# A two-layer transformer block: four tile pairs instead of two at the opening of each FFN, and pools that wait by tile

## The chip, the cores and the metric

The kernel runs on one core of a Trainium2 chip. The metric is the device time of one execution in microseconds; the runs shown are three. The profile is of one further execution.

## The reference

The input is a sequence of 1024 tokens of width 1024 in fp32. Layer 0 mixes with a chunked gMLP and a multi-scale pooling, layer 1 with six heads of differential attention and twelve heads of dilated band attention. Each layer ends in the FFN that the change touches (width 2816), and a final norm closes the block:

```python
def conv_ffn(h, w_up, conv_w, conv_b, w_down):
    a, g = jnp.split(h @ w_up, 2, axis=-1)
    a = lax.conv_general_dilated(a, conv_w, window_strides=(1,), padding=((CONV_WIDTH - 1, 0),),
                                 dimension_numbers=('NWC', 'WIO', 'NWC'), feature_group_count=D_FF) + conv_b
    return (jax.nn.gelu(a) * g) @ w_down
...
        h = h + mix
        h = h + conv_ffn(rms_norm(h, norm_ffn[layer]), ffn_w_up[layer], ffn_conv_w[layer],
                         ffn_conv_b[layer], ffn_w_down[layer])
    return rms_norm(h, final_norm)
```

## The kernel before

Activations are held transposed, features on the 128 partitions and tokens in two halves of 512. Every fp32 operand is split into a high part, rounded by ACT (`A.copy`), and a low part, which DVE subtracts (`V.tensor_sub`); `split` does it for activations, `hi` and `lo` for weights. One product of two 128x128 by 128x512 operands is three matmuls, high by high, low by high and high by low (`mm3`), 512 columns each, added up in one PSUM bank of 128x512 fp32.

**The FFN's up projection** goes over 22 tile pairs j (128 columns of a and of g). Over the two token halves and the two halves of the inner dimension, the eight block products of a pair are brought down to seven (`PRODUCTS`), of 12 matmuls each. Each takes one of four forms of the weights (a itself, two sums of a and g, g itself: `form`, n = 0 to 3) and one operand made from the activations: b11 and b21 from token half 0, and d, e, b22, t3, t4 from sums of both halves. Products 1 and 2 need half 0 alone. Product 1 opens bank x, 2 opens y, 3 opens z; product 4 goes on in x, 5 in z, 6 and 7 in x. Behind a product `read` takes what is needed from the bank: an ACT copy behind 1, 3 and 4, a DVE add behind 2, 5 and 6. `conv` and `gate` close a pair.

**The opening of an FFN.** `out_proj` (and the last projection of the odd mixer in the same way) makes the input h of the FFN tile by tile, with sums of squares for the norm (`Norm.add`). `ff.ahead(i)` makes weight forms early, and `apply(half)` applies the norm: PE adds up over the partitions (ps_n), DVE takes the inverse root (`rsqrt`, twelve small steps n_v to n_rb), PE spreads it over the partitions (ps_b), then DVE scales h and makes the operands: b11 and b21 for half 0, and the seven others for half 1. Then `up` runs products 1 and 2 of pairs 0 and 1, products 3 and 4, 5 and 6, 7 of both, and then pair after pair.

**What sets the order.** Every operation is recorded in program order, and a scheduler lays the records out on the engines by its own estimates; on the chip each engine takes its instructions in that fixed order and waits for semaphores. There are eight PSUM banks: two of pool `ps_mm`, four of `ps_mx`, two of `ps_sm` (norms). In an FFN x takes its bank from `ps_mm`, y and z theirs from `ps_mx`. A pool opened over memory that another pool used makes its first user wait; with `reuse_waits="tile"` it waits for the users of its own bytes, else for the users of the whole pool. The pools of the FFN alone have this mark before. Weight parts come through `wraw_p` (two raw tiles) and `w_tiles` (four pairs of high and low tiles in turn).

Of the kernel before, what the change touches and what calls it, by code (L numbers as in the profile page):

```python
# [60 lines left out]
def tile_block(  # L61
# [22 lines left out]
    const = ctx.enter_context(tc.tile_pool(name="const", bufs=1))  # L84
    dram = ctx.enter_context(tc.tile_pool(name="dram", bufs=1, space=DRAM))
    wraw_p = ctx.enter_context(tc.tile_pool(name="wraw", bufs=2))
    wsp_p = ctx.enter_context(tc.tile_pool(name="wsp", bufs=4))
    hn_p = ctx.enter_context(tc.tile_pool(name="hn", bufs=1))
    ps_mm = ctx.enter_context(tc.tile_pool(name="ps_mm", bufs=2, space=PSUM))
# [174 lines left out]
    class FFN:  # L264
        def __init__(self, layer, stack):
            self.layer = layer
            hp = stack.enter_context(tc.tile_pool(name=f"ffh{layer}", bufs=1, reuse_waits="tile"))
            self.raw_p = stack.enter_context(tc.tile_pool(name=f"ffr{layer}", bufs=4, reuse_waits="tile"))
            self.np = tc.tile_pool(name=f"ffn{layer}", bufs=1, reuse_waits="tile")
# [84 lines left out]
        def form(self, j, n, part):  # L354

            if part == 1:
                return self.lo(j, n)
            if n == 0:
                self.raw(j)
            f = self.forms[j]  # L360
            a, g = f["a"], f["g"]
            c0, c1 = slice(0, HF), slice(HF, S)
            if n == 0:
                self.hi(j, 0, a)
            elif n == 1:
# [2 lines left out]
                V.tensor_add(q[:, c1], q[:, c0], a[:, c0])
# [37 lines left out]
        def read(self, j, n, st):  # L406

            ep = self.ep

            def copy(key, bank):  # L410
                st[key] = ep.tile([P, HF], F32, tag="sb", name=f"f_{key}", bufs=5)
                A.copy(st[key], st[bank])  # L412

            if n == 1:
                copy("x1", "x")
            elif n == 2:
                st["a"] = ep.tile([P, P + S], F32, tag="f_a", name="f_a", bufs=2)
                G.memset(st["a"][:, 0:2], 0.0)
                V.tensor_tensor(st["a"][:, 2 : 2 + HF], st["y"], st["x1"], op=ALU.add)
            elif n == 3:  # L420
                copy("z1", "z")
            elif n == 4:
                copy("u2", "x")
            elif n == 5:
                V.tensor_tensor(st["a"][:, 2 + HF : 2 + S], st["z"], st["u2"], op=ALU.add)
            elif n == 6:
                st["g1"] = ep.tile([P, HF], F32, tag="sb", name="f_g1", bufs=5)
                V.tensor_tensor(st["g1"], st["x"], st["z1"], op=ALU.add)
# [10 lines left out]
        def gate(self, j):  # L439
            st = self.st.pop(j)  # L440
            acc = st["acc"]
            V.scalar_tensor_tensor(acc[:, :HF], acc[:, :HF], -1.0, st["x"], op0=ALU.mult, op1=ALU.mult)
            V.scalar_tensor_tensor(acc[:, HF:], acc[:, HF:], -1.0, st["g1"], op0=ALU.mult, op1=ALU.mult)
            nc.sync.dma_start(a_dram[j], acc)

        def up(self):
            self.st = {}

            both = (0, 1)
            for n in (1, 2):  # L450
                for j in both:
                    self.product(j, n)
# [138 lines left out]
    def odd_mixer():  # L591
        stack = ExitStack()
        with stack:
            ent = stack.enter_context
            qk_p = ent(tc.tile_pool(name="od_qk", bufs=2))
            st_p = ent(tc.tile_pool(name="od_st", bufs=1))
            op = ent(tc.tile_pool(name="od", bufs=1))
            wk = ent(tc.tile_pool(name="od_wk", bufs=2))
            sm = ent(tc.tile_pool(name="od_sm", bufs=4))
            ps_sc = ent(tc.tile_pool(name="ps_sc", bufs=3, space=PSUM))  # L600
            ps_sm = ent(tc.tile_pool(name="ps_s3", bufs=3, space=PSUM))
# [626 lines left out]
```

## Time and profile before

| what | value |
|---|---|
| three runs | 2395.47, 2397.24 and 2398.65 us, median 2397.24 |
| profiled execution | 2396.34 us, span 2394.6, granted clock 0.988 |
| PE | busy 2307.8 us, 96% of the span |
| DVE | busy 1552.0 us, 65% |
| ACT | busy 954.8 us, 40% |
| DMA | 221.60 MB, mean 93 GB/s |
| both FFN openings | about 265 to 305 and 1685 to 1760 us |

A row of the timeline has the start, the duration shown, the engine, the line, the operation, the tiles out and in, and in brackets the idle time before it with what ended it. The duration of a matmul overlaps the next one's, so its cost is read from start to start.

### The profile page before, as it was taken

The page shows a single profiled execution, that of the slowest core. Times are in us where ns is not written, and L with a number is a line of the kernel's source. Part 1 is how long each engine was busy: PE and PEld are TensorE (multiplying, and loading weights), DVE is VectorE, ACT ScalarE, POOL GpSimd, SP SyncE. Part 2 cuts the span into 40 slices and gives each one's busy share as a digit, 9 for nine tenths or more (in the row PEclk, how much of TensorE's full clock was granted, in tenths as well). Part 3 has the DMA queues.
Part 4 walks back from the last instruction along what each step waited for, and adds up shares of the span by engine and source line. Part 5 has one row for each costly group of instructions (what it writes and reads, how often), then busy time and mean ns, then how long its engine had stood idle before and what let it go on. Part 6 is the DMA issues. An engine that isn't in the chain of part 4 may idle for free.

```text
span 2394.6 us, 30695 instructions
## 1 busy us (share of the span) xinstructions
PE 2307.8 (96%) x11652; PEld 1948.4 (81%) x11652; DVE 1552.0 (65%) x2957; ACT 954.8 (40%) x1549; POOL 9.2 (0%) x67
## 2 busy tenths in 40 slices
PE   7999899999999998999999999999699999999997
PEld 7888688888888887898888888878578888888887
DVE  6663976666674447355544788896986666675446
ACT  6231433343441113445544555663444333341111
POOL 0000000000000000000000000000000000000000
PEclk9999999999999999999999999999899999999998
DMA  4114132222273213122122131233322222263211
GB/s 139 62 55 165 36 97 88 79 80 80 88 244 107 89 50 108 55 76 79 60 69 73 37 103 54 75 124 135 134 89 88 88 80 80 86 235 119 88 36 71
DMA packets 174067, 221.60 MB, mean 93 GB/s; under 512 B 11104, under 2 KB 121952, under 8 KB 173920
## 3 DMA queue, kind: packets, MB, share of 16 engines
q1 hardware_dynamic: 173056, 218.61, 28.0%
q8 instruction: 91, 1.49, 0.3%
q10 hardware_dynamic: 864, 1.04, 0.2%
q14 instruction: 56, 0.46, 0.1%
HBM read 160.79 MB, written 52.53 MB: 89 GB/s over the span
## 4 chain that ended last, share of the span: by engine, by line
PE 82%; DVE 9%; ACT 4%; DMA 3%; issue 2%; SPq 0%; DVEq 0%; ACTq 0%
PE ps_d L163 7%; PE ps_d L164 7%; PE ps_d L165 7%; PE ps_x L163 6%; PE ps_x L165 6%; PE ps_x L164 6%; PE ps_z L165 3%; PE ps_z L164 3%; PE ps_z L163 3%; PE ps_qk L163 3%; PE ps_qk L165 3%; PE ps_qk L164 3%; PE ps_o L165 2%; PE ps_o L163 2%; PE ps_o L164 2%
## 5 line engine op out<-in xcount | busy, mean ns | idle before, releaser
L163 PE MATMUL ps_d<-hph,wh 128*128 128x512 f32 (+1 forms) x736 | 279.8, 380 | 0.0
L164 PE MATMUL ps_d<-hpl,wh 128*128 128x512 f32 (+1 forms) x736 | 279.7, 380 | 0.0
L165 PE MATMUL ps_d<-hph,wl 128*128 128x512 f32 (+1 forms) x736 | 279.6, 380 | 0.0
L544 DVE TENSOR_TENSOR x<-ps_d,x 128x512 f32<-128x512 f32 (+1 forms) x200 | 131.9, 666 | 184.9 <-PE ps_d L165 184.7
L134 DVE TENSOR_TENSOR wl<-raw,wh 128x1024 fp32r<-128x1024 f32 (+1 forms) x110 | 131.9, 1200 | 172.7 <-ACT wh L133 172.5
L133 ACT CAST wh<-raw 128x1024 fp32r<-128x1024 f32 (+1 forms) x110 | 113.3, 1036 | 261.8 <-PE ps_d L164 177.3
L348 ACT CAST wh<-q 128x1024 fp32r<-128x1024 f32 x88 | 92.4, 1050 | 247.9 <-PE ps_z L164 218.9
L352 DVE TENSOR_TENSOR wl<-q,wh 128x1024 fp32r<-128x1024 f32 x88 | 107.6, 1224 | 126.7 <-ACT wh L348 126.7
L165 PEld LDWEIGHTS ps_d<-hph,wl 128*128 128x128 f32 x736 | 138.4, 188 | 26.4
L163 PEld LDWEIGHTS ps_d<-hph,wh 128*128 128x128 f32 x736 | 138.4, 188 | 26.3
L164 PEld LDWEIGHTS ps_d<-hpl,wh 128*128 128x128 f32 x736 | 138.4, 188 | 25.9
L163 PE MATMUL ps_qk<-hph,wh 128*128 128x512 f32 x384 | 151.9, 396 | 0.0
L165 PE MATMUL ps_qk<-hph,wl 128*128 128x512 f32 x384 | 151.6, 395 | 0.0
L164 PE MATMUL ps_qk<-hpl,wh 128*128 128x512 f32 x384 | 151.5, 394 | 0.0
L163 PE MATMUL ps_z<-hph,wh 128*128 128x512 f32 x352 | 139.0, 397 | 7.1 <-ACT hph L174 6.6
L163 PE MATMUL ps_x<-x,wh 128*128 128x512 f32 x352 | 137.3, 391 | 4.8 <-ACT f_u L412 4.8
L165 PE MATMUL ps_z<-hph,wl 128*128 128x512 f32 x352 | 139.3, 396 | 1.0 <-DVE wl L352 1.0
L164 PE MATMUL ps_z<-hpl,wh 128*128 128x512 f32 x352 | 139.5, 396 | 0.7 <-DVE hpl L175 0.7
L164 PE MATMUL ps_x<-x,wh 128*128 128x512 f32 x352 | 137.3, 390 | 1.0 <-DVE x L175 1.0
L165 PE MATMUL ps_x<-x,wl 128*128 128x512 f32 x352 | 136.8, 389 | 0.0
L163 PE MATMUL ps_vv<-wh,hph 128*128 128x256 f32 x384 | 110.2, 287 | 10.2 <-ACT qk L660 10.2
L164 PE MATMUL ps_vv<-wl,hph 128*128 128x256 f32 x384 | 110.7, 288 | 0.0
(268 smaller groups left out, 5511.4 us busy)
## 6 DMA issues: line engine op xcount, KB each, us to landing
wr<-in_w_up SPq DMA_DIRECT2D x88, 512.0 KB, 4.1
a_dram<-h SPq DMA_DIRECT2D x44, 512.0 KB, 2.6
ar<-a_dram SPq DMA_DIRECT2D x44, 512.0 KB, 4.6
raw<-in_w_dn SPq DMA_DIRECT2D x44, 512.0 KB, 4.5
raw<-in_w_oin SPq DMA_DIRECT2D x36, 512.0 KB, 3.7
h_dram<-h SPq DMA_DIRECT2D x32, 256.0 KB, 4.8
x<-h_dram SPq DMA_DIRECT2D x32, 256.0 KB, 5.2
raw<-in_w_ein SPq DMA_DIRECT2D x12, 512.0 KB, 4.4
```

Of the source, the lines that this page charges most:

```text
L133: A.copy(wh, raw)
L134: V.tensor_sub(wl, raw, wh.bitcast(F32))
L163: T.matmul(ps, lh, rh, start=first, stop=False, skip_group_check=more)
L164: T.matmul(ps, lh, rl, start=False, stop=False, skip_group_check=more)
L165: T.matmul(ps, ll, rh, start=False, stop=last, skip_group_check=more)
L348: A.copy(t[0], src)
L352: V.tensor_sub(l, src, h.bitcast(F32))
L544: V.tensor_tensor(h, ps, h, op=ALU.add)
```

## The change

Each FFN opens with products 1 and 2 of four tile pairs. `early` names pairs 2 and 3; `ahead(1)` loads their a half once more, ahead of time, and makes form 0 of them, while forms 1 of pairs 0 and 1 are now made in `up`, behind products 1 and 2. The six banks of `ps_mm` and `ps_mx` are taken once and go round in a list (`banks`): a bank comes back to it when y, z or x has been read by DVE. A tile f_s takes the place of f_x, f_z, f_u and f_g, and pairs 2 and 3 keep the sum of y there until ACT copies it into f_a (`open_a`), two copies for each FFN. All pools wait by tile.

```diff
--- before.py
+++ after.py
@@ -81,12 +81,15 @@
     nc = tc.nc
     V, A, G, T = nc.vector, nc.scalar, nc.gpsimd, nc.tensor
 
-    wraw_p = ctx.enter_context(tc.tile_pool(name="wraw", bufs=2))
...
-    ps_mm = ctx.enter_context(tc.tile_pool(name="ps_mm", bufs=2, space=PSUM))
+    def pool(name, **kw):
+        return tc.tile_pool(name=name, reuse_waits="tile", **kw)
+
+    wraw_p = ctx.enter_context(pool(name="wraw", bufs=2))
...
+    ps_mm = ctx.enter_context(pool(name="ps_mm", bufs=2, space=PSUM))
 
 
     ident = const.tile([P, P], F32, name="ident")
@@ -338,10 +341,12 @@
 
         def raw(self, j):
             f = self.forms[j] = {}
-            src = w_up[self.layer, j].rearrange("p (k x c) -> p k x c", x=2, c=P)
             for i, x in enumerate("ag"):
                 f[x] = self.raw_p.tile([P, 1024], F32, tag="wr", name="wr")
-                nc.sync.dma_start(f[x].rearrange("p (k c) -> p k c", c=P), src[:, :, i, :])
+                nc.sync.dma_start(f[x].rearrange("p (k c) -> p k c", c=P), self.columns(j, i))
+
+        def columns(self, j, i):
+            return w_up[self.layer, j].rearrange("p (k x c) -> p k x c", x=2, c=P)[:, :, i, :]
 
         def hi(self, j, n, src):
             t = self.forms[j][n] = [x[:, : src.shape[-1]] for x in w_tiles()] + [src]
@@ -355,7 +360,7 @@
 
             if part == 1:
                 return self.lo(j, n)
-            if n == 0:
+            if j not in self.forms or n == 1 and j in self.early:
                 self.raw(j)
             f = self.forms[j]
             a, g = f["a"], f["g"]
@@ -379,9 +384,19 @@
             self.form(j, n, 0)
             self.form(j, n, 1)
 
+        early = (2, 3)
+
         def ahead(self, i):
-            for j in range(2):
-                self.forms_of(j, i)
+
+            for j in (2 * i, 2 * i + 1):
+                if j not in self.early:
+                    self.forms_of(j, 0)
+                    continue
+                a = wraw_p.tile([P, 1024], F32, tag="raw", name="a")
+                nc.sync.dma_start(a.rearrange("p (k c) -> p k c", c=P), self.columns(j, 0))
+                self.forms[j] = {}
+                self.hi(j, 0, a)
+                self.lo(j, 0)
 
 
         PRODUCTS = {
@@ -394,8 +409,7 @@
             tile_n, block, b, opens = self.PRODUCTS[n]
             bank = {2: "y", 3: "z", 5: "z"}.get(n, "x")
             if opens:
-                st[bank] = ps_mm.tile([P, HF], F32, tag="mm", name="ps_x") if n == 1 else ps_mx.tile(
-                    [P, HF], F32, tag="mx", name=f"ps_{bank}")
+                st[bank] = self.banks.pop(0)
             wh, wl, _ = self.forms[j][tile_n]
             bh, bl = self.B[b]
             for k in range(4):
@@ -406,26 +420,30 @@
         def read(self, j, n, st):
 
             ep = self.ep
-
-            def copy(key, bank):
-                st[key] = ep.tile([P, HF], F32, tag="sb", name=f"f_{key}", bufs=5)
-                A.copy(st[key], st[bank])
-
-            if n == 1:
-                copy("x1", "x")
+            if n in (1, 3):
+                st[n] = ep.tile([P, HF], F32, tag="sb", name=f"f_s{n}", bufs=6)
+                A.copy(st[n], st["x" if n == 1 else "z"])
             elif n == 2:
-                st["a"] = ep.tile([P, P + S], F32, tag="f_a", name="f_a", bufs=2)
-                G.memset(st["a"][:, 0:2], 0.0)
-                V.tensor_tensor(st["a"][:, 2 : 2 + HF], st["y"], st["x1"], op=ALU.add)
-            elif n == 3:
-                copy("z1", "z")
+
+                if j not in self.early:
+                    self.open_a(j)
+                to = st[1] if j in self.early else st["a"][:, 2 : 2 + HF]
+                V.tensor_tensor(to, st["y"], st[1], op=ALU.add)
+                self.banks.append(st["y"])
             elif n == 4:
-                copy("u2", "x")
+                A.copy(st[1], st["x"])
             elif n == 5:
-                V.tensor_tensor(st["a"][:, 2 + HF : 2 + S], st["z"], st["u2"], op=ALU.add)
+                V.tensor_tensor(st["a"][:, 2 + HF : 2 + S], st["z"], st[1], op=ALU.add)
+                self.banks.append(st["z"])
             elif n == 6:
-                st["g1"] = ep.tile([P, HF], F32, tag="sb", name="f_g1", bufs=5)
-                V.tensor_tensor(st["g1"], st["x"], st["z1"], op=ALU.add)
+                V.tensor_tensor(st[3], st["x"], st[3], op=ALU.add)
+
+        def open_a(self, j):
+            st = self.st[j]
+            st["a"] = self.ep.tile([P, P + S], F32, tag="f_a", name="f_a", bufs=2)
+            G.memset(st["a"][:, 0:2], 0.0)
+            if j in self.early:
+                A.copy(st["a"][:, 2 : 2 + HF], st[1])
 
         def conv(self, j):
             st, a = self.st[j], self.st[j]["a"]
@@ -440,16 +458,24 @@
             st = self.st.pop(j)
             acc = st["acc"]
             V.scalar_tensor_tensor(acc[:, :HF], acc[:, :HF], -1.0, st["x"], op0=ALU.mult, op1=ALU.mult)
-            V.scalar_tensor_tensor(acc[:, HF:], acc[:, HF:], -1.0, st["g1"], op0=ALU.mult, op1=ALU.mult)
+            self.banks.append(st["x"])
+            V.scalar_tensor_tensor(acc[:, HF:], acc[:, HF:], -1.0, st[3], op0=ALU.mult, op1=ALU.mult)
             nc.sync.dma_start(a_dram[j], acc)
 
         def up(self):
             self.st = {}
+            self.banks = [ps_mm.tile([P, HF], F32, tag="mm", name=f"ps_u{i}") for i in range(2)]
+            self.banks += [ps_mx.tile([P, HF], F32, tag="mx", name=f"ps_u{i + 2}") for i in range(4)]
 
             both = (0, 1)
-            for n in (1, 2):
-                for j in both:
-                    self.product(j, n)
+            for j in both:
+                self.product(j, 1)
+                self.product(j, 2)
+            for j in both:
+                self.forms_of(j, 1)
+            for j in self.early:
+                self.product(j, 1)
+                self.product(j, 2)
             for j in both:
                 self.forms_of(j, 2)
             for n in (3, 4):
@@ -462,8 +488,8 @@
                     self.product(j, n)
                     if n == 5:
                         self.conv(j)
-                    else:
-                        self.forms_of(2, j)
+                    elif j == 1:
+                        self.forms_of(2, 1)
             for j in both:
                 self.product(j, 7)
                 self.gate(j)
@@ -472,13 +498,17 @@
                 nxt = j + 1 if j + 1 < NFF else None
 
                 def form(n, part):
-                    if nxt is not None:
+                    if nxt is not None and not (n == 0 and nxt in self.early):
                         self.form(nxt, n, part)
 
-                self.product(j, 1)
+                if j in self.early:
+                    self.open_a(j)
+                else:
+                    self.product(j, 1)
                 if j > 2:
                     self.form(j, 3, 1)
-                self.product(j, 2)
+                if j not in self.early:
+                    self.product(j, 2)
                 if j > 2:
                     self.gate(j - 1)
                 form(0, 0)
...
@@ -592,13 +622,13 @@
-            qk_p = ent(tc.tile_pool(name="od_qk", bufs=2))
-            ps_sc = ent(tc.tile_pool(name="ps_sc", bufs=3, space=PSUM))
+            qk_p = ent(pool(name="od_qk", bufs=2))
+            ps_sc = ent(pool(name="ps_sc", bufs=3, space=PSUM))
...
```

PE in the second FFN, around the spreading of the norm (ps_b). In ps_x, ps_y, ps_z the letter names the bank's use; ps_u0 to ps_u5 are the six banks; hph and hpl are operands b11, b21 (half 0: _0) and d, b22 (_1), x_0 and x_1 are parts of e. Before:

```order
L209 MATMUL ps_n_14732<-narrow_77,nsum_14631 128x1 x4
L218 MATMUL ps_b_14754<-ident_72,n_rb_14752 128x128 x4
L163 MATMUL ps_z_14877<-hph_0_1_83,wh_14721 128x512
L163 MATMUL ps_z_14892<-hph_0_1_83,wh_14728 128x512
L164 MATMUL ps_z_14877<-hpl_0_1_91,wh_14721 128x512
...
L163 MATMUL ps_z_14877<-hph_1_1_85,wh_14721 128x512
...
L163 MATMUL ps_x_14803<-x_0_0_14599,wh_14721 128x512
L163 MATMUL ps_x_14818<-x_0_0_14599,wh_14728 128x512
...
L164 MATMUL ps_x_14803<-x_1_0_14601,wh_14721 128x512
```

and now:

```order
L168 MATMUL ps_u5_14708<-hph_3_0_88,wl_14623 128x512
L221 MATMUL ps_b_14654<-ident_72,n_rb_14652 128x128 x4
L166 MATMUL ps_u0_14703<-x_0_0_14501,wh_14770 128x512
L166 MATMUL ps_u2_14705<-x_0_0_14501,wh_14777 128x512
L167 MATMUL ps_u0_14703<-x_1_0_14503,wh_14770 128x512
...
L167 MATMUL ps_u2_14705<-x_1_0_14503,wh_14777 128x512
...
L167 MATMUL ps_u0_14703<-x_1_1_14504,wh_14770 128x512
...
L166 MATMUL ps_u1_14704<-hph_0_0_82,wh_14628 128x512
...
L166 MATMUL ps_u3_14706<-hph_2_0_86,wh_14628 128x512
...
L166 MATMUL ps_u5_14708<-hph_0_1_83,wh_14770 128x512
```

Ahead of the change product 3 (hph_0_1 into ps_z) of pairs 0 and 1 stood behind ps_b, and product 4 (x_0_0 into ps_x) behind it. Now product 4 stands there, then products 1 and 2 of pair 3 on the banks u1 and u3, which held y of pairs 0 and 1, and then product 3.

DVE in the second FFN, at the end of apply(1), before:

```order
L335 SCALAR_TENSOR_TENSOR h_3_0_14428<-h_1_0_14424,h_3_0_14428 128x1024
L175 TENSOR_TENSOR h_2_1_14791<-h_2_0_14426,h_0_1_14789 128x1024
L419 TENSOR_TENSOR f_a_14846<-ps_y_14833,f_x1_14816 128x512
L175 TENSOR_TENSOR h_3_1_14792<-h_3_0_14428,h_1_1_14790 128x1024
L419 TENSOR_TENSOR f_a_14862<-ps_y_14849,f_x1_14831 128x512
L352 TENSOR_TENSOR wl_14936<-wr_14558,wh_14935 128x512
```

and now:

```order
L338 SCALAR_TENSOR_TENSOR h_3_0_14330<-h_1_0_14326,h_3_0_14330 128x1024
L178 TENSOR_TENSOR h_2_1_14691<-h_2_0_14328,h_0_1_14689 128x1024
L431 TENSOR_TENSOR f_a_14735<-ps_u1_14704,f_s1_14721 128x512
L178 TENSOR_TENSOR h_3_1_14692<-h_3_0_14330,h_1_1_14690 128x1024
L431 TENSOR_TENSOR f_a_14764<-ps_u3_14706,f_s1_14750 128x512
L431 TENSOR_TENSOR f_s1_14793<-ps_u5_14708,f_s1_14793 128x512
```

The adds that read y of pairs 0 and 1 (L419, now L431) kept their place in the queue, between and behind the last low halves; one more, for pair 2, came behind them.

PE in the first FFN, around ps_b, before:

```order
L164 MATMUL ps_y_2370<-hpl_3_0_96,wh_2183 128x512
L218 MATMUL ps_b_2291<-ident_72,n_rb_2289 128x128 x4
L165 MATMUL ps_y_2370<-hph_3_0_88,wl_2184 128x512
...
L165 MATMUL ps_y_2386<-hph_3_0_88,wl_2192 128x512
L163 MATMUL ps_z_2414<-hph_0_1_83,wh_2258 128x512
L163 MATMUL ps_z_2429<-hph_0_1_83,wh_2265 128x512
L164 MATMUL ps_z_2414<-hpl_0_1_91,wh_2258 128x512
...
L163 MATMUL ps_x_2340<-x_0_0_2095,wh_2258 128x512
```

and now:

```order
L167 MATMUL ps_u3_2341<-hpl_3_0_96,wh_2191 128x512
L221 MATMUL ps_b_2289<-ident_72,n_rb_2287 128x128 x4
L168 MATMUL ps_u3_2341<-hph_3_0_88,wl_2192 128x512
...
L166 MATMUL ps_u4_2342<-hph_0_0_82,wh_2257 128x512
...
L166 MATMUL ps_u5_2343<-hph_2_0_86,wh_2257 128x512
...
L166 MATMUL ps_u0_2338<-x_0_0_2095,wh_2405 128x512
L166 MATMUL ps_u2_2340<-x_0_0_2095,wh_2412 128x512
L167 MATMUL ps_u0_2338<-x_1_0_2097,wh_2405 128x512
...
L166 MATMUL ps_u1_2339<-hph_0_0_82,wh_2263 128x512
...
L166 MATMUL ps_u3_2341<-hph_2_0_86,wh_2263 128x512
...
L166 MATMUL ps_u5_2343<-hph_0_1_83,wh_2405 128x512
```

Before, ps_b stood one matmul ahead of the end of pair 0's product 2 (ps_y_2370), with pair 1's (ps_y_2386) behind it. Now it stands within pair 1's product 2 (ps_u3); products 1 and 2 of pair 2 (u4, u5) come behind, and then the order is as in the second FFN.

More of the change, by code (lines that the diff above doesn't have):

```diff
@@ L82, in tile_block @@
     V, A, G, T = nc.vector, nc.scalar, nc.gpsimd, nc.tensor
[L84 to L89 removed]
+    def pool(name, **kw):
+        return tc.tile_pool(name=name, reuse_waits="tile", **kw)
+    const = ctx.enter_context(pool(name="const", bufs=1))
+    dram = ctx.enter_context(pool(name="dram", bufs=1, space=DRAM))
+    wraw_p = ctx.enter_context(pool(name="wraw", bufs=2))
+    wsp_p = ctx.enter_context(pool(name="wsp", bufs=4))
+    hn_p = ctx.enter_context(pool(name="hn", bufs=1))
+    ps_mm = ctx.enter_context(pool(name="ps_mm", bufs=2, space=PSUM))
     ident = const.tile([P, P], F32, name="ident")
@@ L266, in __init__ @@
             self.layer = layer
-            hp = stack.enter_context(tc.tile_pool(name=f"ffh{layer}", bufs=1, reuse_waits="tile"))
-            self.raw_p = stack.enter_context(tc.tile_pool(name=f"ffr{layer}", bufs=4, reuse_waits="tile"))
-            self.np = tc.tile_pool(name=f"ffn{layer}", bufs=1, reuse_waits="tile")
+            hp = stack.enter_context(pool(name=f"ffh{layer}", bufs=1))
+            self.raw_p = stack.enter_context(pool(name=f"ffr{layer}", bufs=4))
+            self.np = pool(name=f"ffn{layer}", bufs=1)
             self.tile = lambda x, m, h, t: hp.tile([P, 2, HF], t, tag=f"{x}{m}{h}", name=f"{x}_{m}_{h}")
@@ L562, in run @@
             self.np.__exit__(None, None, None)
-            with tc.tile_pool(name=f"ffe{self.layer}", bufs=1, reuse_waits="tile") as self.ep:
+            with pool(name=f"ffe{self.layer}", bufs=1) as self.ep:
                 self.up()
-            with tc.tile_pool(name=f"ffm{self.layer}", bufs=1, reuse_waits="tile") as np_:
+            with pool(name=f"ffm{self.layer}", bufs=1) as np_:
                 norm = Norm(np_)
@@ L594, in odd_mixer @@
             ent = stack.enter_context
-            qk_p = ent(tc.tile_pool(name="od_qk", bufs=2))
[L596 to L599, printed above, removed]
-            ps_sc = ent(tc.tile_pool(name="ps_sc", bufs=3, space=PSUM))
-            ps_sm = ent(tc.tile_pool(name="ps_s3", bufs=3, space=PSUM))
+            qk_p = ent(pool(name="od_qk", bufs=2))
+            st_p = ent(pool(name="od_st", bufs=1))
+            op = ent(pool(name="od", bufs=1))
+            wk = ent(pool(name="od_wk", bufs=2))
+            sm = ent(pool(name="od_sm", bufs=4))
+            ps_sc = ent(pool(name="ps_sc", bufs=3, space=PSUM))
+            ps_sm = ent(pool(name="ps_s3", bufs=3, space=PSUM))
             cosT = op.tile([P, HF], F32, name="cosT")
@@ L961, in tile_block @@
     banks = ExitStack()
-    ps_mx = banks.enter_context(tc.tile_pool(name="ps_mx0", bufs=4, space=PSUM))
-    ps_sm = banks.enter_context(tc.tile_pool(name="ps_sm0", bufs=2, space=PSUM))
+    ps_mx = banks.enter_context(pool(name="ps_mx0", bufs=4, space=PSUM))
+    ps_sm = banks.enter_context(pool(name="ps_sm0", bufs=2, space=PSUM))
     QT = HF // 2
     even = ExitStack()
-    evr = even.enter_context(tc.tile_pool(name="ev_r", bufs=1))
+    evr = even.enter_context(pool(name="ev_r", bufs=1))
     r_row = [evr.tile([P, HF], F32, name=f"r_row{h}") for h in range(2)]
@@ L973, in tile_block @@
         for q in range(4):
-            xp = x0.enter_context(tc.tile_pool(name=f"x{q}", bufs=1))
+            xp = x0.enter_context(pool(name=f"x{q}", bufs=1))
             xt.append([xp.tile([P, QT], F32, name=f"x_{q}_{kt}") for kt in range(KT)])
-        nrm = Norm(x0.enter_context(tc.tile_pool(name="x_n", bufs=1)))
+        nrm = Norm(x0.enter_context(pool(name="x_n", bufs=1)))
         for q in range(4):
@@ L993, in tile_block @@
             V.tensor_copy(r_col[:, q * 2 : q * 2 + 2], y[:, :2])
-    with tc.tile_pool(name="ev_v", bufs=1) as evv, tc.tile_pool(name="ev", bufs=1) as ev, tc.tile_pool(
+    with pool(name="ev_v", bufs=1) as evv, pool(name="ev", bufs=1) as ev, pool(
         name="ev2", bufs=2
@@ L1130, in tile_block @@
     with ExitStack() as stack:
-        ps_mx = stack.enter_context(tc.tile_pool(name="ps_mx1", bufs=4, space=PSUM))
-        ps_sm = stack.enter_context(tc.tile_pool(name="ps_sm1", bufs=2, space=PSUM))
+        ps_mx = stack.enter_context(pool(name="ps_mx1", bufs=4, space=PSUM))
+        ps_sm = stack.enter_context(pool(name="ps_sm1", bufs=2, space=PSUM))
         ff = FFN(1, stack)
```

## The prediction

> **What bounds the kernel now.** I read the page's busy shares and its chain of waits first, then windows of 60 us side by side, then the rows of PE, DVE and ACT in the windows that fall short. The rows are the busy line, the chain's shares by engine, and three windows: the opening of the first FFN, the opening of the second, and a steady stretch of an FFN (columns: PE, PEld, DVE, ACT, POOL busy us and count, granted clock, DMA share, GB/s).
>
> ```profile
> PE 2307.8 (96%) x11652; PEld 1948.4 (81%) x11652; DVE 1552.0 (65%) x2957; ACT 954.8 (40%) x1549; POOL 9.2 (0%) x67
> PE 82%; DVE 9%; ACT 4%; DMA 3%; issue 2%; SPq 0%; DVEq 0%; ACTq 0%
> 240.00:300.00 60.00, 50.73 (x216) 39.33 (x216) 55.32 (x84) 26.71 (x32) 0.36 (x2) 0.94 0.11 36
> 1680.00:1740.00 60.00, 41.28 (x164) 32.24 (x164) 56.73 (x90) 26.04 (x32) 0.20 (x2) 0.80 0.33 109
> 1800.00:1860.00 60.00, 60.00 (x267) 49.67 (x266) 38.91 (x47) 23.18 (x28) 0.30 (x3) 1.00 0.25 79
> ```
>
> PE sets the end wherever it has work: the steady window is full, and 267 matmuls in it give about 0.227 us each, start to start. The two openings are the places where PE waits, and there DVE is the busy one (55.32 and 56.73 of 60). So the change is worth what it does to PE's waits in two stretches, at about 265 to 305 us and 1705 to 1760 us. First PE in the second opening (a bracket is idle time before the row and what ended it; the last two rows group 1705 to 1760 by line, with the idle time behind the second bar):
>
> ```profile
> 1706.25 1.02 PE L209 MATMUL ps_n<-narrow,nsum 128*128 128x1 f32 x8 [1.28 <-DVE nsum L202]
> 1715.37 2.04 PE L218 MATMUL ps_b<-ident,n_rb 128*128 128x128 f32 x8 [8.09 <-DVE n_rb L215]
> 1722.20 1.22 PE L163 MATMUL ps_z<-hph,wh 128*128 128x512 f32 x2 [4.79 <-ACT hph L174]
> 1725.02 0.63 PE L164 MATMUL ps_z<-hpl,wh 128*128 128x512 f32 x1
> 1726.30 0.63 PE L163 MATMUL ps_z<-hph,wh 128*128 128x512 f32 x1
> 1727.31 0.40 PE L164 MATMUL ps_z<-hpl,wh 128*128 128x512 f32 x1
> 1754.62 0.50 PE L163 MATMUL ps_x<-h,wh 128*128 128x512 f32 x1 [1.00 <-DVE f_g L428]
> ...
> L163 PE MATMUL ps_z<-hph,wh 128*128 128x512 f32 x17 | 7.8, 469 | 5.2 <-ACT hph L174 4.8 <-ACT wh L348 0.5
> L164 PE MATMUL ps_z<-hpl,wh 128*128 128x512 f32 x17 | 7.5, 442 | 0.2 <-DVE hpl L175 0.2
> ```
>
> The matmuls of products 1 and 2 for two tile pairs end at 1704.97 (1706.25 less 1.28). PE then waits 1.28 + 8.09 + 5.2 + 0.2 + 1.00 = 15.8 us. After a wait matmuls start 0.43 us apart (1725.02 to 1726.30 is three steps), until about 1726.9, ten of them: a slow stretch costs 10 x 0.20 = 2.0 us. ps_b itself took 2.04 where the warm one below takes 1.05. In all 15.8 + 2.0 + 1.0 = 18.8 us are lost here. Now what DVE and ACT do at that time:
>
> ```profile
> 1705.43 0.68 DVE L202 TENSOR_TENSOR nsum<-nsum,nsq 128x512 f32<-128x512 f32 x1
> 1706.03 0.68 DVE L368 TENSOR_TENSOR q<-q,wr 128x512 f32<-128x512 f32 x1
> 1707.32 0.16 DVE L212 TENSOR_SCALAR n_v<-ps_n 128x4 f32<-128x4 f32 x1 [0.60 <-PE ps_n L209]
> 1714.80 0.42 DVE L215 COPY n_rb<-n_y 128x512 f32<-128x512 f32 x1
> 1717.88 2.06 DVE L309 SCALAR_TENSOR_TENSOR h<-h,narrow,ps_b 128x512 f32<-128x512 f32 x3
> 1729.96 1.21 DVE L175 TENSOR_TENSOR x<-h,x 128x1024 fp32r<-128x1024 f32 x1
> 1734.50 1.21 DVE L175 TENSOR_TENSOR x<-h,x 128x1024 fp32r<-128x1024 f32 x1
> 1742.45 0.68 DVE L419 TENSOR_TENSOR f_a<-ps_y,f_x 128x512 f32<-128x512 f32 x1
> 1744.18 0.67 DVE L419 TENSOR_TENSOR f_a<-ps_y,f_x 128x512 f32<-128x512 f32 x1
> 1728.28 1.06 ACT L174 CAST x<-h 128x1024 fp32r<-128x1024 f32 x1 [1.59 <-DVE h L326]
> ```
>
> Call D the start of the first scaling behind ps_b (L309, 1717.88). From D on DVE works through apply(1) without a pause. The operand of product 4 has its high half at D+11.5 (1728.28 + 1.06), its low halves at D+13.3 (1729.96 + 1.21) and D+17.8 (1734.50 + 1.21). The two adds that read the y banks end at D+25.25 and D+27.0. Before the change nobody waits for these adds, since products 3 and 4 have banks of their own.
>
> **The change part by part, second FFN.** It adds 24 matmuls of tile pair 2 ahead of ps_b and 24 of pair 3 behind it; they are moved from later, PE's count is the same. There are six banks. Pairs 0, 1 and 2 take all six, and pair 3 opens on the banks of y of pairs 0 and 1, that is behind the two adds, which DVE still has at the end of its apply(1) queue. Behind pair 3 in PE's order stands product 3 of pairs 0 and 1, which ran at D+4.3 before. So three things move.
>
> (a) ps_n stands behind 16 of the moved matmuls: 1704.97 + 16 x 0.227 = 1708.6, so n_v comes at 1709.7 in place of 1707.32. Between n_v and n_rb DVE now has one 128x512 add more (0.6 us, 1705.43 to 1706.03). n_rb and D move by 2.4 + 0.6 = 3.0 us, D to 1720.9. PE is busy to 1704.97 + 5.45 + 1.02 = 1711.4 and waits to 1718.4 (1715.37 + 3.0): 6.9 us, and 1.0 for a slow ps_b.
>
> (b) From ps_b's end (1720.4) PE has two matmuls until D+13.3, at 1734.2: 13.3 us of waiting and a slow stretch of 2.0. The rest of product 4 (22 matmuls, ten of them slow) then runs to D+20.3; the second low half at D+17.8 is in time.
>
> (c) From D+20.3 to D+25.25 PE waits for pair 0's y bank: 4.95, and 2.0 for slow matmuls. Then 48 matmuls run without a stop; the second bank (D+27.0) is in time.
>
> Sum 6.9 + 1.0 + 13.3 + 2.0 + 4.95 + 2.0 = 30.2 against 18.8: **+11.4 us**. From below: D does not move (-3) and neither wait makes matmuls slow (-4), +4.4. From above: DVE's forms wait for casts once more (1 us), and the y add of pair 3 or a late weight costs one 128x1024 step or two (1.2 each), +15.
>
> **First FFN.** PE, DVE and ACT in its opening, and the window of its loss:
>
> ```profile
> 269.33 1.05 PE L218 MATMUL ps_b<-ident,n_rb 128*128 128x128 f32 x8
> 275.20 0.73 PE L163 MATMUL ps_z<-hph,wh 128*128 128x512 f32 x2 [1.86 <-ACT hph L174]
> 288.65 0.50 PE L164 MATMUL ps_x<-x,wh 128*128 128x512 f32 x1 [1.02 <-DVE x L175]
> 296.74 0.78 PE L163 MATMUL ps_x<-x,wh 128*128 128x512 f32 x1 [4.00 <-ACT f_u L412]
> 298.93 0.80 PE L165 MATMUL ps_z<-hph,wl 128*128 128x512 f32 x1 [0.98 <-DVE wl L352]
> 272.00:305.00 33.00, 23.86 (x79) 16.88 (x79) 30.86 (x33) 14.87 (x18) 0.00 (x0) 0.84 0.08 25
> 264.83 0.16 DVE L212 TENSOR_SCALAR n_v<-ps_n 128x4 f32<-128x4 f32 x1 [0.90 <-PE ps_n L209]
> 268.62 0.43 DVE L215 COPY n_rb<-n_y 128x512 f32<-128x512 f32 x1
> 270.42 2.06 DVE L309 SCALAR_TENSOR_TENSOR h<-h,narrow,ps_b 128x512 f32<-128x512 f32 x3 [1.37 <-PE ps_b L218]
> 282.84 1.22 DVE L175 TENSOR_TENSOR x<-h,x 128x1024 fp32r<-128x1024 f32 x1
> 287.38 1.22 DVE L175 TENSOR_TENSOR x<-h,x 128x1024 fp32r<-128x1024 f32 x1
> 295.33 0.68 DVE L419 TENSOR_TENSOR f_a<-ps_y,f_x 128x512 f32<-128x512 f32 x1
> 296.10 0.58 ACT L412 COPY f_u<-ps_x 128x512 f32<-128x512 f32 x1 [0.69 <-DVE f_a L419]
> ```
>
> Lost before: 33.0 - 79 x 0.227 = 15.1 us. After it, D = 270.42 moves: between n_v and n_rb DVE gets one low split more (1.2) and two adds (0.6 each), and I allow 0.3 for a weight cast that has to wait for its buffer: 2.7 in all, D = 273.1. Here pair 2's 24 matmuls and the last 4 of pair 1 stand behind ps_b: 28 x 0.227 = 6.4, to D+6.4. Then PE waits for product 4's low half (282.84 + 1.22, D+13.6) with two matmuls between: 6.8, and 2.0 slow; for the second low half (D+18.2) 1.6; then from D+19.6 for the y bank (295.33 + 0.68, D+25.6) 6.0, and 2.0 slow; 0.4 ahead of ps_b. Sum 18.8, less 15.1: **+3.7 us**. The 4.00 wait for f_u goes, since the f_ copies get six slots and no new one is taken there. From below, with no slow matmuls behind the two waits, 0; from above, with a second cast wait moving D by two steps and the first 24 matmuls late by as much, +8.
>
> The clock can be weighed otherwise. The Trainium skill ("TensorE: Matmul & The Clock Gate", Part 1, What's actually happening) has it that a cold start lasts about 3.4 us by a free-running window, with 6 to 14 slow matmuls seen. By that page four stretches of 1.2 to 2.8 us would make the whole sum about 3 us less or more; the trace's ten matmuls, 2.0 us, lie in between and are used.
>
> **What is hidden.** Two 512 KB loads of a weight half for each FFN issue well ahead, where the DMA share is 0.11 to 0.33; uncovered, one would delay a cast, in the upper ends above. Two ACT copies more for each FFN, of the size of f_u, lie on an engine that is busy 26 of 60 us: 0, and 1.2 us uncovered. **Pools that wait by tile**: the largest wait beside a pool is the one ahead of attention.
>
> ```profile
> 961.97 0.58 PE L163 MATMUL ps_vv<-wh,hph 128*128 128x256 f32 x1 [10.17 <-ACT qk L660]
> 960.81 0.62 ACT L174 CAST hph<-n_t 128x512 fp32r<-128x512 f32 x1 [0.82 <-DVE n_t L227]
> 961.34 1.06 ACT L660 COPY qk<-ps_qk 128x512 f32<-128x512 f32 x2
> ```
>
> The copy comes right behind ACT's last cast of the norm, and in ACT's order it stands behind it after the change too. So the pool's wait frees nothing: 0, and 0.8 us of gain as the bound (one wait of the norm, 0.82).
>
> Total +11.4 + 3.7 = +15.1. The profiled execution took 2396.34 (span 2394.6 and 1.74 around it), 0.9 below the median of 2397.24: 2411.4 there, **2412 us** as a median. The ends: +4.4 + 0 - 0.8 = +3.6 and +15 + 8 = +23, from 2400 to 2420.
>
> **The rivals.**
>
> *The added products fill the waits* (faster). If pair 3's matmuls too ran in the idle time, 48 x 0.227 = 10.9 us would go into the 8.09 + 4.79 of the second FFN, and the waits 1.86 + 1.02 + 4.00 + 0.98 = 7.9 of the first would be filled: 2397.2 - 18.8 = 2378. For it: the idle time is there. Against it: the banks, freed at D+25; and product 3, the work that fills D+4.3 to D+11.5 today, stands behind them. It decides if the y adds run before apply(1). The Trainium skill ("Perfetto Trace Analysis", Optimizing Tensor Performance, Matmuls) says that independent groups should rotate through banks so that the emptying of one overlaps the next group's matmuls, which is what this rival counts on; in the steady window the trace agrees, 60.00 of 60 with the banks in rotation. Chance 0.08.
>
> *DVE sets the end of the opening anyway* (no change). DVE is busy 56.73 of 60 and the change moves its instructions without adding any; if PE's later work waits for DVE to empty its queue, what PE misses costs nothing: 2397. Against it: behind 1744 PE runs full (60.00 of 60), so matmuls owed at D+25 are paid for. Chance 0.08.
>
> *The pools free the attention's start*: 10.2 less, 2412 - 10.2 = 2402. Against it ACT's order. Chance 0.06.
>
> **How the numbers follow.** Forecast 0.78, rivals 0.08, 0.08 and 0.06. The range 2400 to 2420 holds the forecast with its bounds and the third rival, about 8 in 10. Under 0.2% (4.8 us) this measurement can't tell a change: faster 0.09 (the first rival and a rest), same 0.11 (the second and half of the third), slower 0.80.
>
> **What would show it.** In the profile after: a wait of about 13 us on PE behind ps_b in the second opening, ended by the low half of x, then one of about 5 ended by DVE's add at L431 ahead of ps_u; in the first opening two waits of about 6 to 7 with the same enders; n_rb 3 us later against the rows around it; the 10.17 us ahead of ps_vv unchanged. I am wrong if pair 3's matmuls start before D+20, if product 3 runs ahead of them, or if the window from D+30 on still has waits that hide the loss.

## The result and the profile after

The changed kernel takes 2411.35 us in the median (2410.45 to 2413.09), the kernel before 2397.8 (2395.47 to 2398.65). The ratio is 1.0059 with a 95% interval of 1.0042 to 1.0076: slower by 0.6%, 14 us. One execution among all those below, in the run with three pairs and two banks emptied by ACT, took 9481 us and is left out of its ratio. The profiled executions differ by as much, with spans of 2408.7 and 2394.6.

The windows of the two openings, of the kernel after. The second window is taken 4 us later than the same one of before, since the same row of DVE (the last of the four low halves of half 0, L178) starts 4.14 us later there; columns as in the prediction.

```profile
262.00:322.00 60.00, 46.56 (x188) 36.53 (x187) 46.82 (x66) 21.25 (x26) 0.00 (x0) 0.86 0.13 40
1700.00:1770.00 70.00, 46.56 (x184) 37.00 (x184) 54.13 (x76) 25.89 (x31) 0.00 (x0) 0.80 0.10 31
```

and of the kernel before:

```profile
262.00:322.00 60.00, 50.86 (x206) 39.42 (x205) 54.44 (x74) 25.59 (x31) 0.56 (x4) 0.91 0.19 60
1696.00:1766.00 70.00, 54.24 (x226) 42.90 (x225) 65.97 (x89) 35.07 (x41) 0.40 (x4) 0.88 0.20 60
```

PE gets through 18 matmuls less in the first opening and 42 less in the second. At 0.227 us these are 4.1 and 9.5 us. In the whole run PE and DVE have the same instructions as before and ACT four copies more; here each is less busy. PE's lost time is the time from the start of each matmul to the next one's, less what it takes at full speed. Added up over all matmuls of the trace it grows from 15.7 to 20.4 us in the first opening (240 to 400 us), from 28.1 to 38.5 in the second (1675 to 1900), and falls by 1.0 in all the rest: 14.1.

PE in the second opening, after:

```profile
1712.33 0.95 PE L212 MATMUL ps_n<-narrow,nsum 128*128 128x1 f32 x8
1721.66 2.05 PE L221 MATMUL ps_b<-ident,n_rb 128*128 128x128 f32 x8 [6.42 <-DVE n_rb L218]
1735.25 1.22 PE L166 MATMUL ps_u<-x,wh 128*128 128x512 f32 x2 [11.54 <-ACT x L177]
1737.10 0.79 PE L167 MATMUL ps_u<-x,wh 128*128 128x512 f32 x1 [0.63 <-DVE x L178]
1749.05 0.80 PE L166 MATMUL ps_u<-hph,wh 128*128 128x512 f32 x1 [4.86 <-DVE f_a L431]
```

and DVE at the same time:

```profile
1703.08 1.22 DVE L178 TENSOR_TENSOR hpl<-h,hph 128x1024 fp32r<-128x1024 f32 x1
1713.31 0.16 DVE L215 TENSOR_SCALAR n_v<-ps_n 128x4 f32<-128x4 f32 x1 [1.92 <-PE ps_n L212]
1721.08 0.43 DVE L218 COPY n_rb<-n_y 128x512 f32<-128x512 f32 x1
1723.74 2.06 DVE L312 SCALAR_TENSOR_TENSOR h<-h,narrow,ps_b 128x512 f32<-128x512 f32 x3 [2.23 <-PE ps_b L221]
1748.32 0.68 DVE L431 TENSOR_TENSOR f_a<-ps_u,f_s 128x512 f32<-128x512 f32 x1
1757.46 0.69 DVE L431 TENSOR_TENSOR f_s<-ps_u,f_s 128x512 f32<-128x512 f32 x1 [4.80 <-PE ps_u L168]
```

Here D is 1723.74. The add of pair 0's y starts at D+24.6, 1748.32, at the end of DVE's queue of apply(1), and PE takes up pair 3 in that bank as soon as it is through. Later DVE itself waits 4.80 us for PE (the last row): what PE did not do in time, DVE cannot read.

The first opening, after, on PE:

```profile
271.53 1.13 PE L221 MATMUL ps_b<-ident,n_rb 128*128 128x128 f32 x8 [0.25 <-DVE n_rb L218]
284.40 1.22 PE L166 MATMUL ps_u<-x,wh 128*128 128x512 f32 x2 [5.38 <-ACT x L177]
290.80 0.50 PE L167 MATMUL ps_u<-x,wh 128*128 128x512 f32 x1 [1.19 <-DVE x L178]
298.21 0.80 PE L166 MATMUL ps_u<-hph,wh 128*128 128x512 f32 x1 [5.99 <-DVE f_a L431]
```

The same two waits: for product 4's operand, then for the bank that DVE's add holds.

### The profile page after: what moved, and what is told of

Read it like the earlier page. It is cut to its first block, busy times and chain, and to the rows that moved or that the text cites. A ratio compares the mean times of both kernels' runs of the same rounds, so it can differ in the third digit from the quotient of the medians.

```text
span 2408.7 us, 30648 instructions
## 1 busy us (share of the span) xinstructions
PE 2309.5 (96%) x11652; PEld 1950.2 (81%) x11652; DVE 1551.8 (64%) x2957; ACT 958.4 (40%) x1553; POOL 9.4 (0%) x67
## 4 chain that ended last, share of the span: by engine, by line
PE 82%; DVE 8%; ACT 4%; DMA 3%; issue 2%; SPq 0%; DVEq 0%; ACTq 0%
PE ps_u L166 12%; PE ps_u L168 12%; PE ps_u L167 12%; PE ps_d L166 6%; PE ps_d L167 6%; PE ps_d L168 6%; PE ps_qk L167 3%; PE ps_qk L168 3%; PE ps_qk L166 3%; PE ps_o L166 2%; PE ps_o L168 2%; PE ps_o L167 2%; PE ps_vv L166 2%; PE ps_vv L168 2%; PE ps_vv L167 2%
## 5 line engine op out<-in xcount | busy, mean ns | idle before, releaser
L166 PE MATMUL ps_u<-hph,wh 128*128 128x512 f32 x768 | 302.2, 394 | 14.4 <-DVE f_a L431 10.8
L168 PE MATMUL ps_u<-hph,wl 128*128 128x512 f32 x768 | 301.9, 393 | 0.3 <-DVE wl L357 0.3
L167 PE MATMUL ps_u<-hpl,wh 128*128 128x512 f32 x768 | 301.7, 393 | 0.0
L166 PEld LDWEIGHTS ps_u<-hph,wh 128*128 128x128 f32 x768 | 146.1, 190 | 45.6 <-DVE f_a L431 11.7
L168 PEld LDWEIGHTS ps_u<-hph,wl 128*128 128x128 f32 x768 | 145.7, 190 | 31.2 <-DVE wl L357 0.8
L167 PEld LDWEIGHTS ps_u<-hpl,wh 128*128 128x128 f32 x768 | 146.0, 190 | 30.6
L166 PE MATMUL ps_u<-x,wh 128*128 128x512 f32 x352 | 138.7, 396 | 16.9 <-ACT x L177 16.9
L167 PE MATMUL ps_u<-x,wh 128*128 128x512 f32 x352 | 138.9, 395 | 2.4 <-DVE x L178 2.4
```

What stands on the lines that cost most here:

```text
L166: T.matmul(ps, lh, rh, start=first, stop=False, skip_group_check=more)
L167: T.matmul(ps, lh, rl, start=False, stop=False, skip_group_check=more)
L168: T.matmul(ps, ll, rh, start=False, stop=last, skip_group_check=more)
```

## The experiments

The theory: three pairs take all six banks, so the next product that opens one has to take a bank of y, which DVE empties at the end of its queue of apply(1); in PE's fixed order that product, and product 3 behind it, hold up the rest. The rivals: the pools; the amount of work that is moved forward, with what it adds to DVE ahead of n_rb; the copies and the list of banks. Each run has its median, and beside it the kernel before was run on the same chip; the ratio is of these two sets of runs, with its 95% interval, and can differ in the last digits from that of the medians.

### The pools alone

The kernel before, with `reuse_waits="tile"` on every pool:

```diff
+    def pool(name, **kw):
+        return tc.tile_pool(name=name, reuse_waits="tile", **kw)
-    const = ctx.enter_context(tc.tile_pool(name="const", bufs=1))
+    const = ctx.enter_context(pool(name="const", bufs=1))
...
```

> Only the pools: the kernel before, with every pool waiting by tile; the FFN openings as before. My theory (the loss is made in the two openings, by the order of PE around ps_b): no difference, 2397 to 2399 us, and the 10.17 us wait of PE ahead of ps_vv stays. The rival that the pools cost time or give it back: 2392 or less if they free the start of attention or of the even mixer, 2404 or more if they carry part of the 14 us.

Measured: 2398.29 us, ratio 1.0007 (0.9999 to 1.0016). The wait ahead of attention, in this run:

```profile
963.12 0.58 PE L166 MATMUL ps_vv<-wh,hph 128*128 128x256 f32 x1 [10.19 <-ACT qk L663]
```

It is as long as before (10.17): the pool's wait was behind ACT's order and freed nothing. The pools are worth nothing that can be told.

### The opening alone

```diff
     def pool(name, **kw):
-        return tc.tile_pool(name=name, reuse_waits="tile", **kw)
+        if name.startswith("ff"):
+            kw["reuse_waits"] = "tile"
+        return tc.tile_pool(name=name, **kw)
```

> Only the opening: the changed kernel with the pools outside the FFN waiting by whole pool again. My theory: all of the loss stays, 2410 to 2413. The rival that pools carry part: nearer to 2398 by that part.

Measured: 2413.03 us, ratio 1.0068 (1.0055 to 1.0080). The whole loss is in the opening; this and the run of the pools give the two parts of the change apart.

### Two pairs, with the list of banks

The changed kernel with the opening narrowed:

```diff
-        early = (2, 3)
+        early = ()
...
                 if j not in self.early:
-                    self.forms_of(j, 0)
+                    if j < 2:
+                        self.forms_of(j, 0)
                     continue
...
-                    elif j == 1:
-                        self.forms_of(2, 1)
+                    elif j == 1 or 2 not in self.early:
+                        self.forms_of(2, j)
```

> The changed kernel with two pairs at the opening instead of four; the six banks still go round in a list, and forms 1 are still made behind products 1 and 2. With two pairs the list gives product 3 two banks that were never used (u4, u5), and in PE's order it stands right behind ps_b, as before. My theory: the 13 us wait behind ps_b is gone (about 5 as before), and what is left is DVE's forms ahead of n_rb: 2397 to 2402. The rival that the list of banks or the copies themselves cost the time: 2408 or more.

Measured: 2397.68 us, ratio 0.9999 (0.9990 to 1.0007): as before. Its second opening on PE:

```profile
1715.42 2.05 PE L221 MATMUL ps_b<-ident,n_rb 128*128 128x128 f32 x8 [6.90 <-DVE n_rb L218]
1722.87 1.22 PE L166 MATMUL ps_u<-hph,wh 128*128 128x512 f32 x2 [5.40 <-ACT hph L177]
```

Product 3 (hph into a bank not used yet) is back behind ps_b, and the wait there is 5.40 in place of 11.54. The list, the f_s tiles and the later forms 1 together cost nothing that can be told.

### Three pairs

The same with `early = (2,)`: half of the added products, and all six banks taken.

> The changed kernel with three pairs at the opening. Pair 3 is not opened early any more, so half of the added products is gone; but three pairs take all six banks, and product 3 of pairs 0 and 1 now has to take the banks of y (u1, u3) and wait for DVE's adds at about 25 us behind D. My theory (a bank that DVE empties late, with product 3 behind it): the loss stays nearly whole, 2408 to 2413. The rival that the loss grows with the amount of work moved forward (24 matmuls of each FFN instead of 48): about half, 2403 to 2406.

Measured: 2406.75 us, ratio 1.0041 (1.0027 to 1.0055). It lies between the two expectations, a bit above the one of half the work and a bit below mine. The rows show why:

```profile
1720.14 1.83 PE L221 MATMUL ps_b<-ident,n_rb 128*128 128x128 f32 x8 [4.72 <-DVE n_rb L218]
1733.51 1.22 PE L166 MATMUL ps_u<-x,wh 128*128 128x512 f32 x2 [11.55 <-ACT x L177]
1747.32 0.50 PE L166 MATMUL ps_u<-hph,wh 128*128 128x512 f32 x1 [4.13 <-DVE f_a L432]
```

The wait behind ps_b is the same to 0.01 us (11.55), with 24 matmuls fewer moved: this is no matter of the amount. The third row is now product 3, waiting for the same add. What is smaller is the wait ahead of ps_b (4.72 for 6.42), where DVE has one low split less, and the one for the bank. So the bank carries most of the loss, and DVE's work ahead of n_rb some 2 us of it.

### Three pairs, with two banks emptied by ACT

ACT copies y of pairs 0 and 1 into f_a, and DVE adds x1 there, in place:

```diff
                 to = st[1] if j in self.early else st["a"][:, 2 : 2 + HF]
-                V.tensor_tensor(to, st["y"], st[1], op=ALU.add)
+                y = st["y"]
+                if j < 2:
+                    A.copy(to, y)
+                    y = to
+                V.tensor_tensor(to, y, st[1], op=ALU.add)
                 self.banks.append(st["y"])
```

> Three pairs at the opening, and y of pairs 0 and 1 is copied out of its bank by ACT (into f_a, where DVE adds x1 later, in place), so that the bank comes free without DVE's queue. Product 3 takes the same banks u1 and u3 as in the run with three pairs; PE's order puts it right behind ps_b again. One ACT copy of 0.58 us more for each of two pairs in each FFN, DVE's count unchanged. My theory: the waits at 13 us and 25 us behind D go, pair 2's 24 matmuls lie in PE's idle time: about 4 us better than before in the second FFN and 7 to 10 in the first, 2383 to 2390. The rival that DVE's work (D moved by 2 to 3 us) or the number of early pairs makes the loss: no better than before, 2398 to 2406.

Measured: 2393.70 us, ratio 0.9981 (0.9972 to 0.9990), 13 us better than the run with three pairs and faster than before, though by less than I expected. PE in its second opening, and the largest wait of its first:

```profile
1715.12 2.05 PE L221 MATMUL ps_b<-ident,n_rb 128*128 128x128 f32 x8 [4.72 <-DVE n_rb L218]
1721.54 1.22 PE L166 MATMUL ps_u<-hph,wh 128*128 128x512 f32 x2 [4.37 <-ACT hph L177]
1743.14 0.58 PE L166 MATMUL ps_u<-x,wh 128*128 128x512 f32 x1 [2.25 <-ACT f_s L439]
...
298.37 0.80 PE L166 MATMUL ps_u<-x,wh 128*128 128x512 f32 x1 [5.45 <-ACT f_s L439]
```

The pairs' number, the wait ahead of ps_b and DVE's count are those of the run with three pairs; only who empties y has changed, and with it PE's order. The waits of 11.55 and 4.13 are gone, and behind ps_b 4.37 is left, where the kernel before had 4.79. This is the test of the theory, and it holds. The gain I expected beyond it is held by the last two rows: product 6 waits for the copy behind product 4.

### Four pairs, with two banks emptied by ACT

The same edit on the changed kernel itself.

> Four pairs as in the change, and y of pairs 0 and 1 copied out by ACT. Pair 3's products 1 and 2 can run right behind ps_b; but product 3 of pair 0 takes u5, the bank of pair 2's y, which DVE still empties at about 28 us behind D, and product 3 of pair 1 the bank of pair 3's y. My theory: the wait behind ps_b shrinks by the 5.4 us of pair 3 and a wait of 7 to 10 us ahead of product 3 stays, in all 2400 to 2406. The rival that emptying two banks is enough for four pairs: 2390 or less.

Measured: 2404.99 us, ratio 1.0029 (1.0019 to 1.0038). The time is the expected one, and pair 3 runs behind ps_b, but the second wait is another than I named. PE in its second opening:

```profile
1733.99 1.22 PE L166 MATMUL ps_u<-x,wh 128*128 128x512 f32 x2 [5.33 <-ACT x L177]
1748.47 0.79 PE L166 MATMUL ps_u<-x,wh 128*128 128x512 f32 x1 [5.53 <-ACT f_s L438]
```

The second row is the start of product 6, which waits for the copy behind product 4 (L438); this copy goes over a tile that DVE's late add still reads. Product 3 (hph) comes behind it in PE's order, from 1750.34 on, when the first of DVE's two adds from the banks of pairs 2 and 3 (from 1749.39 on) is through. So DVE's late adds hold PE here too, but through the f_s tile first; how long the banks alone would have held it was not run.

### The copy behind product 4, out of the way

That copy goes over the tile of x1, which DVE's late add still has to read. Here it goes into the second half of f_a:

```diff
             elif n == 4:
-                A.copy(st[1], st["x"])
+                A.copy(st["a"][:, 2 + HF : 2 + S], st["x"])
             elif n == 5:
-                V.tensor_tensor(st["a"][:, 2 + HF : 2 + S], st["z"], st[1], op=ALU.add)
+                V.tensor_tensor(st["a"][:, 2 + HF : 2 + S], st["z"], st["a"][:, 2 + HF : 2 + S], op=ALU.add)
```

Three kernels had this edit: the run above with three pairs, the kernel before (where f_u waits 4.00 us in the same way), and the changed kernel.

> As the run with three pairs and y emptied by ACT, but the ACT copy behind product 4 goes into the second half of f_a instead of over the tile that holds x1. In that run PE still waited 5.45 and 0.57 us in the first FFN and 2.25 in the second for an ACT copy into f_s; that copy waits for DVE's add of y and x1, which reads the same tile at about 25 us behind D. My theory (DVE's late add is the root, first by the bank and then by the f_s tile): these waits and their slow matmuls go, 8 to 10 us better than 2393.7, 2382 to 2387. The rival that DVE's remaining queue holds PE anyway: 2391 or more.

Measured: 2394.59 us, ratio 0.9985 (0.9977 to 0.9994): no better. My theory fell here, and the trace says why:

```profile
302.49 0.80 PE L168 MATMUL ps_u<-hph,wl 128*128 128x512 f32 x1 [6.33 <-DVE wl L357]
```

The wait for the copy is gone, and PE waits as long for the low half of form 2, which is next in DVE's queue behind apply(1). The rival was right: it is the queue's end that holds PE there, whatever it reads first.

> The kernel before with this one edit: the copy behind product 4 (f_u) goes into the second half of f_a and takes no tile of its own. In the first FFN of before PE waits 4.00 us, and matmuls are slow for 2 us behind it, because f_u gets its tile only when DVE's add has read f_x. My theory: that wait goes, 4 to 7 us better, 2390 to 2394, with nothing to win in the second FFN, which has no such wait. The rival that another wait at the same place takes over: 2396 to 2398.

Measured: 2395.73 us, ratio 0.9991 (0.9983 to 1.0000): some 2 us, at most 4 by the interval, and below the rival's range by 0.3. The same again:

```profile
297.89 0.80 PE L165 MATMUL ps_z<-hph,wl 128*128 128x512 f32 x1 [5.72 <-DVE wl L352]
```

4.00 and 0.98 of the kernel before have become one wait of 5.72, so nothing is gained there: added up from start to start, PE loses as much in both openings as before, to within 0.3 us.

> The changed kernel (four pairs, y added by DVE) with the same edit of the copy behind product 4. In the changed kernel PE waits for the banks of y, not for an f_s tile. My theory: nothing to win, 2409 to 2412. The rival that the f_s tile (its six slots) is part of the change's loss: 2406 or less.

Measured: 2406.94 us, ratio 1.0033 (1.0021 to 1.0046), some 4 to 6 us better than the change. I had expected nothing. PE in its second opening:

```profile
1737.19 1.22 PE L166 MATMUL ps_u<-x,wh 128*128 128x512 f32 x2 [11.55 <-ACT x L177]
1751.00 0.50 PE L166 MATMUL ps_u<-hph,wh 128*128 128x512 f32 x1 [1.45 <-DVE f_a L431]
```

The wait for y's bank has shrunk from 4.86 to 1.45. Once the copy is free of the add, the scheduler puts product 6 of pair 0 (12 matmuls, 2.7 us) ahead of pair 3. So in the change the f_s tile took part after all: it kept the one product that could have run meanwhile behind the bank.

### Four pairs, with all four banks emptied by ACT

The changed kernel, with y of pairs 0 and 1 copied into f_a, y of pairs 2 and 3 into a tile of their own, and the copy behind product 4 in f_a:

```diff
+                y = st["y"]
+                if j in self.early:
+                    y = ep.tile([P, HF], F32, tag="sb", name="f_y", bufs=6)
+                    A.copy(y, st["y"])
+                elif j < 2:
+                    A.copy(to, y)
+                    y = to
-                V.tensor_tensor(to, st["y"], st[1], op=ALU.add)
+                V.tensor_tensor(to, y, st[1], op=ALU.add)
```

> Four pairs as in the change, with all four y banks emptied by ACT (of pairs 2 and 3 into a tile f_y of their own, within the six f_s slots) and the copy behind product 4 in f_a. DVE's adds of y are where they were, at the end of apply(1), but they read no bank. In PE's order stand then, behind ps_b: pair 3's products 1 and 2, product 3 of pairs 0 and 1 and product 4, each with a free bank. My theory (a bank that waits for DVE's queue, not the four pairs, makes the change slow): this is faster than before, and than the run with three pairs and two banks emptied (2393.7): 2386 to 2393. It still waits some 3 us for the slot of f_x at about 25 us behind D. The rival that four pairs cost more on DVE (two more low splits ahead of n_rb) than they bring on PE: 2396 or more.

Measured: 2391.31 us, ratio 0.9974 (0.9965 to 0.9984). It is the fastest of all, 0.26% faster than before and 20 us faster than the change. PE in its second opening:

```profile
1714.80 2.04 PE L221 MATMUL ps_b<-ident,n_rb 128*128 128x128 f32 x8 [6.41 <-DVE n_rb L218]
1725.97 0.50 PE L166 MATMUL ps_u<-hph,wh 128*128 128x512 f32 x1 [0.50 <-ACT hph L177]
1735.83 0.50 PE L167 MATMUL ps_u<-x,wh 128*128 128x512 f32 x1 [1.26 <-DVE x L178]
1743.86 0.50 PE L166 MATMUL ps_u<-hph,wh 128*128 128x512 f32 x1 [1.18 <-ACT f_s L425]
1756.67 0.50 PE L166 MATMUL ps_u<-h,wh 128*128 128x512 f32 x1 [1.78 <-DVE f_s L446]
```

In the second opening no wait from ps_b on is longer than 1.3 us, up to the last row, 1.78 for an add in DVE's queue. In the first one a wait of 3.83 is left, for an ACT copy into an f_s tile, which itself waits for DVE's late add:

```profile
298.76 0.79 PE L166 MATMUL ps_u<-hph,wh 128*128 128x512 f32 x1 [3.83 <-ACT f_s L425]
```

The 6.41 ahead of ps_b is as in the change (6.42): it is DVE's chain to n_rb, and emptying banks does nothing for it. By start-to-start sums the first opening loses 11.8 us (15.7 before) and the second 27.1 (28.1). That the second gains so little goes with DVE's chain ahead of ps_b and the adds behind apply(1), to which PE now comes sooner. The same four copies without the edit of the copy behind product 4 were not run, so the two parts of this gain are not told apart.

## Why the prediction was right

**The total**: +15.1 was forecast, +14.1 in the spans and 13.6 in the medians came. None of the three signs of being wrong showed: pair 3's matmuls start at D+25.3 (1749.05), product 3 stands behind them, and from D+30 to 1790 us the longest wait of PE is 0.65.

**(a), D in the second opening.** n_rb was to move by 3.0 us. Against the row at 1703.08 (1698.94 before, so 4.14 to take off) it moved by 2.1 (1721.08 - 4.14, against 1714.80), and D by 1.7. I sized it too high: ps_n came 0.4 us sooner than my count, and the stretch from n_v to n_rb grew by 0.3 (7.48 to 7.77) in place of 0.6. Before the change D also stood another half microsecond behind ps_b's end, for two adds (L367, L368) that are now elsewhere. The rows of the kernel before:

```profile
1698.94 1.22 DVE L175 TENSOR_TENSOR hpl<-h,hph 128x1024 fp32r<-128x1024 f32 x1
1717.27 0.69 DVE L368 TENSOR_TENSOR q<-q,wr 128x512 f32<-128x512 f32 x1
```

The wait ahead of ps_b was 6.42, 6.9 in the sum.

**(b) and (c).** From ps_b's end (1723.71) to the low half of x (1737.10) 13.4 us passed, in the sum 13.8; the wait for y's bank was 4.86, in the sum 4.95. The enders are the ones named. The second opening came to +10.4 in place of +11.4; of the difference 0.5 is the wait ahead of ps_b and 0.4 the shorter way from ps_b to x, both from (a).

**The first opening.** Waits of 0.25, 5.38 + 0.63, 1.19 and 5.99 stand for 0.4, 6.8, 1.6 and 6.0; the second was 0.8 smaller. These waits come to 13.4 where the sum has 14.8, and still the opening was dearer than forecast, +4.7 in place of +3.7. It lost 20.4 us against the 18.8 of the sum. The 0.6 us by which before's whole loss (15.7) is above my 15.1 do not explain this: with them alone the forecast would have been lower. What was mis-sized is the slow matmuls and the restarts behind the waits: the sum has 4.0 for them, and if those 0.6 us are lost after the change as well, 6.4 are left for them by difference. The errors in the two openings, -1.0 and +1.0, cancel; that the total comes so close is luck in this part.

**Slow matmuls.** 2.0 us for a stretch was a little low: the twelve matmuls behind the wait for the bank in the second opening (last section) cost 2.6 us more than at 0.227 us each.

**The rivals.** That the added products fill the waits was priced at 2378. It needed the banks, and with the banks given (the last run) it gave 2391: the price left out that DVE's queue then ends what the banks ended before, and that DVE's chain ahead of ps_b stays (6.41 us). The rival that DVE sets the end anyway is wrong for the change, where owed matmuls were paid in full; but it is what stopped the repairs of the copy. The pools freed nothing: 10.19 us ahead of ps_vv remains.

**One step was right only in part.** "The f_ copies get six slots and no new one is taken there", so f_u's wait goes: it went from the list of waits, but the copy into f_s still came only behind DVE's add, and kept product 6 behind pair 3. The run with that copy in f_a shows this as some 4 to 6 us of the change's loss. I had put all of it down to the bank.

## What to carry to other kernels

Work that is moved forward into an idle stretch takes buffers with it; ask for each buffer which engine gives it back, and what stands ahead of that instruction in the engine's queue. In an engine with a fixed order, one product that waits for a bank holds up those behind it that could run. Where two engines can empty a bank, let the idle one do it: ACT copies of 0.58 us that empty the banks ahead of the adds at the end of DVE's queue, with one more copy moved out of the way, turned 14 us lost into 6 won.

## What the runs showed of the hardware

A stretch of slow matmuls behind a wait has no fixed length. In the kernel after, behind the wait of 4.86 us, matmuls start 0.43 us apart from the second on (the first step is 0.60):

```profile
1749.65 0.63 PE L167 MATMUL ps_u<-hpl,wh 128*128 128x512 f32 x1
...
1753.91 0.63 PE L168 MATMUL ps_u<-hph,wl 128*128 128x512 f32 x1
1754.34 0.48 PE L166 MATMUL ps_u<-hph,wh 128*128 128x512 f32 x1
```

It is 5.3 us and twelve matmuls from 1749.05 to 1754.34. In the run with three pairs, behind 4.13 us, the first step is 0.33 us, and the slow ones end 3.7 us after the first start:

```profile
1747.65 0.59 PE L167 MATMUL ps_u<-hpl,wh 128*128 128x512 f32 x1
1748.04 0.63 PE L168 MATMUL ps_u<-hph,wl 128*128 128x512 f32 x1
...
1751.03 0.43 PE L166 MATMUL ps_u<-hph,wh 128*128 128x512 f32 x1
```

The Trainium skill ("TensorE: Matmul & The Clock Gate", Part 1, What's actually happening) says that the activity window runs free and that the number of slow matmuls therefore varies, with 6, 11 and 14 seen for one kernel; twelve and eight lie in that range.
